# A hybrid trunk layer on one core: other planner prices, a later start for small parameters, halved state products, and FFN groups of 4, 6, 6 and 6

## The chip, the cores and the metric

One core of a Trainium2 chip runs the whole program in one launch. The metric is the device time in microseconds (us). Before the change three runs gave 1941.99, 1941.85 and 1940.84, a median of 1941.85. A separate profiled execution took 1942.22, of which the trace's span is 1940.5.

## The reference

One layer of a streaming encoder works on 640 tokens of width 1024: 512 prompt tokens of one request and 16 new tokens of each of 8 others, with the same weights:

```
x += 0.5 * swiglu(rmsnorm(x), w_ffn1_up, w_ffn1_down)      # up 1024 -> 2*2816, down 2816 -> 1024
P  = rmsnorm(x) @ w_in                                     # 1024 -> 10752 columns
A  = sliding-window attention, 16 heads, 4 kv heads, QK norm, a learned sink per head
B  = HGRN2 recurrence, 8 heads, state 128 x 128 per head and request
C  = causal conv(4) -> RG-LRU scan, times GeLU gate
x += (sig(gA)*A@w_attn_o + sig(gB)*B@w_hgrn_o + sig(gC)*C@w_lru_o) @ w_out
x += 0.5 * swiglu(rmsnorm(x), w_ffn2_up, w_ffn2_down)
```

Outputs are x, new keys and values, and the new HGRN2, convolution and RG-LRU states of both groups. All of it is float32. For HGRN2's sample requests the state update per head is `S = exp(b) * S + K^T V` over that request's 16 tokens.

## The kernel before

Activations lie transposed, features on the partitions and 640 tokens along the row, in two halves of 320. Every large product is taken three times: a weight is split into a high part `wh` and a remainder `wl` of the fast type (f32r), the activation likewise, and `wh`·high, `wh`·low, `wl`·high are added in PSUM (`proj`; the split is the cast in L717 and the subtraction in L718). So one 128-column block of weights takes 8 × 3 × 2 = 48 matmuls of 128x320. Small products (head products, HGRN2's, transposes in `tr`, L427) are plain f32 on the same engine; the program counts as a *kind* the type and the number of output rows.

The SwiGLU (`ffn`) runs over 22 blocks of 128 hidden columns. The first group of six computes gate and up plainly (2 × 48 = 96 matmuls a block). The later groups use seven products of combined halves in place of eight (`pair`, 84 matmuls a block), on sums and differences of the input that `combos` makes; `combos` is called after block 2 and finished at the end of the first group. After each group the down-projection goes over the 8 output blocks with the group's hidden blocks as contraction (`f0, nf` in the loop), and adds into x.

At the start `load_x` brings x in, transposes it, scales and splits it into `RA`; squares on ScalarE give the row sums, `first_rstd` the scale `RS`, which is applied after the first products. `load_params` brings the norm gains, biases and similar vectors as rows of one tile `AR`, transposes them once and copies them to `PRM`. `SK` holds the attention sinks, broadcast along the partitions by ten transfers; one DVE operation in `attention` negates them. `RA` and `RB` are the split operands of up- and down-projection.

The order is not the code's: every operation is put on a list with a priority (its position, `item`, less a `lag` for loads and splits), and `Sched.run` plays the five engines with modelled durations: the earliest start wins, ties within 0.04 go by priority, on ScalarE a function whose table isn't loaded pays `LOAD` after it has been picked. What comes out is one fixed program for each engine. An engine takes its instructions in that order, and a wait holds up all that stand behind it. DMAs go through SP's one queue.

Of the kernel before, what the change touches and what calls it, by code (L numbers as in the profile page):

```python
# [152 lines left out]
class Op:  # L153
    __slots__ = ("alts", "prio", "npred", "succ", "ready", "news", "bufs", "func", "dma", "done")


class Sched:
# [103 lines left out]
    def run(self):  # L261
# [3 lines left out]
        loaded, dma_free = "none", 0.0  # L265
# [70 lines left out]
def trunk_kernel(ctx: ExitStack, tc: tile.TileContext, A: dict, O: list):  # L336
# [65 lines left out]
    def dma(out, a, lag=None):  # L402
        v = out if isinstance(out, View) else a
        return S.op([("SP", 0.47, lambda: nc.sync.dma_start(ap_of(out), ap_of(a)))], [a], [out],  # L404
                    dma=v.n * 4 * v.proto.shape[0], lag=lag)

    def mm(calls):

        def cost(o, l, m):
# [11 lines left out]
        return S.op([("PE", dur, f)], [x for c in calls for x in c[1:3]], [c[0] for c in calls])  # L421

    def tr(calls):
# [5 lines left out]
        return S.op([("PE", sum(0.002 + 0.835e-3 * c[0].n for c in calls), f)], [x for c in calls for x in c[1:]], [c[0] for c in calls])  # L429
# [110 lines left out]

    def load_x():
        bs = S.buf("xs")
        xin = []
        for c in range(4):
            b = S.buf("x0")
            v = b.v.r("p (t d) -> p t d", t=4)
            dma(v, xp[:, :, c * 256:(c + 1) * 256], lag=(12, 2.5, 1.9, 1.8)[c])
# [4 lines left out]
        xv = X.v.r("p (k t) -> p k t", k=KD)
        for c in range(4):
# [31 lines left out]
    def load_params(names, r0, r1, lag=None):  # L585
        b = S.buf("pst")
        for name, r, c in (("norm_ffn1", 0, 8), ("norm_mix", 8, 8), ("norm_ffn2", 16, 8), ("conv_b", 24, 8),
                           ("conv_w", 32, 32), ("lru_b_a", 64, 8), ("lru_b_x", 72, 8), ("lru_lambda", 80, 8),
                           ("hgrn_lb_logits", 88, 8), ("hgrn_o_norm", 96, 1)):
            if name in names:  # L590
                src = A[name][0].rearrange("j (k p) -> (j k) p", p=P) if name == "conv_w" else A[name].rearrange("o (k p) -> (o k) p", p=P)
                dma(b[r - r0:r - r0 + c, 0:P].at(r), src, lag=lag)
        for r, name in ((97, "q_norm"), (98, "k_norm")):
            if name in names:
                for h in range(2):
                    dma(b[r - r0:r - r0 + 1, h * 64:h * 64 + 64].at((r, h)), A[name], lag=lag)
        ps = S.buf("ml")
        n = r1 - r0
        tr([(ps[:, :n], b[:n, :P], ident[:n, :n])])
        cp(PRM[:, r0:r1].at(r0), ps[:, :n], only=("DVE",))  # L600
# [257 lines left out]
    def ffn(wu, wd, norm, R, H, sfx, done, aside=()):  # L858
        ops = None
        for f0, nf in ((0, 6), (6, 8), (14, 8)):  # L860
            for f in range(nf):
# [16 lines left out]
            for m in range(KD):
# [338 lines left out]
    def hgrn():  # L1217
        mk = S.buf("msk")
        M1, BM, PM = mk[:, 0:32], mk[:, 112:120], mk[:, 120:122]
# [25 lines left out]
        S.op([("POOL", 0.2, lambda: nc.gpsimd.iota(il[:, 0:8](), [[-16, 8]], base=0, channel_multiplier=1))], (), [il[:, 0:8]])  # L1245
        ts(il[:, 0:8], il[:, 0:8], 4, ALU.arith_shift_right, only=one)
        ts(BM, il[:, 0:8], 0.0, ALU.is_equal, only=one)
# [14 lines left out]
        def head(i):  # L1262
# [186 lines left out]
```

## Time and profile before

| | |
|---|---|
| median of three runs | 1941.85 us |
| profiled execution | 1942.22 us, span 1940.5 us, mean granted clock 0.996 |
| TensorE (PE) | busy 1907.8 us, 98% |
| VectorE (DVE) | busy 1359.5 us, 70% |
| ScalarE (ACT) | busy 743.8 us, 38%, of which 127.0 us are 99 table loads |
| GpSimd (POOL) | busy 25.3 us |
| HBM traffic | 143.32 MB read, 10.63 MB written, 79 GB/s |

The profile gives busy time by engine, groups of equal instructions with their count and mean duration, the waits with what ended them, and a chain followed back from the last instruction. A matmul's record overlaps the next one's, so the time of one is read from the number in a full stretch and not from its own record. The granted clock is a share of full speed. With TensorE at 98%, places where it is idle, slow or does other work are what there is to find.

### The profile page before, as it was taken

The page shows a single profiled execution, that of the slowest core. Times are in us where ns is not written, and L with a number is a line of the kernel's source. Part 1 is how long each engine was busy: PE and PEld are TensorE (multiplying, and loading weights), DVE is VectorE, ACT ScalarE, POOL GpSimd, SP SyncE. Part 2 cuts the span into 40 slices and gives each one's busy share as a digit, 9 for nine tenths or more (in the row PEclk, how much of TensorE's full clock was granted, in tenths as well). Part 3 has the DMA queues.
Part 4 walks back from the last instruction along what each step waited for, and adds up shares of the span by engine and source line. Part 5 has one row for each costly group of instructions (what it writes and reads, how often), then busy time and mean ns, then how long its engine had stood idle before and what let it go on. Part 6 is the DMA issues. An engine that isn't in the chain of part 4 may idle for free.

```text
span 1940.5 us, 35075 instructions
## 1 busy us (share of the span) xinstructions
PE 1907.8 (98%) x14702; PEld 1862.7 (96%) x14702; DVE 1359.5 (70%) x2531; ACT 743.8 (38%) x1278; POOL 25.3 (1%) x58
## 2 busy tenths in 40 slices
PE   6999999999999999999999999999999999999999
PEld 5999999999999999989999999999999999999998
DVE  4957947866778783778547787886566867956963
ACT  4324513422478840887102343434212213412420
POOL 0000000000000000000000000000000000000000
PEclk9999999999999999999999999999999999999999
DMA  4223332234322212212322232222422223222322
GB/s 128 81 68 88 88 87 73 81 91 133 90 66 56 63 53 73 72 53 80 88 77 68 84 89 74 81 83 68 135 77 73 70 76 98 80 84 77 87 73 70
DMA packets 304440, 156.87 MB, mean 81 GB/s; under 512 B 22645, under 2 KB 301782, under 8 KB 304282
## 3 DMA queue, kind: packets, MB, share of 16 engines
q1 hardware_dynamic: 304282, 154.63, 27.6%
q8 instruction: 115, 1.88, 0.4%
q14 instruction: 43, 0.35, 0.1%
HBM read 143.32 MB, written 10.63 MB: 79 GB/s over the span
## 4 chain that ended last, share of the span: by engine, by line
PE 93%; DVE 3%; ACT 2%; SPq 1%; DMA 1%; issue 0%; DVEq 0%; ACTq 0%
PE pp L419 84%; PE me L419 4%; PE ml L419 3%; PE ml L427 1%; SPq L404 1%; PE me L427 1%; ACT L383 1%; DVE AR L373 1%; ACT AR L383 1%; DMA SK<-in_attn_sinks_dram 1%; DVE AR L359 1%; DVE wl L718 0%; DVE AR L1188 0%; DVE RB L359 0%; DVE wh L717 0%
## 5 line engine op out<-in xcount | busy, mean ns | idle before, releaser
L419 PE MATMUL pp<-RA,wh 128*128 128x320 f32 x4288 | 837.1, 315 | 4.2 <-DVE AR L359 3.9
L419 PEld LDWEIGHTS pp<-RA,wh 128*128 128x128 f32 x4288 | 674.8, 189 | 15.3 <-issue 7.6
L419 PE MATMUL pp<-RA,wl 128*128 128x320 f32 x2144 | 500.7, 310 | 1.1 <-DVE wl L718 1.1
L419 PE MATMUL pp<-RB,wh 128*128 128x320 f32 x2112 | 404.9, 309 | 1.4 <-DVE AR L359 0.9
L419 PEld LDWEIGHTS pp<-RA,wl 128*128 128x128 f32 x2144 | 362.6, 189 | 1.9 <-DVE wl L718 1.9
L419 PEld LDWEIGHTS pp<-RB,wh 128*128 128x128 f32 x2112 | 333.9, 188 | 2.2 <-DVE AR L359 1.4
L717 DVE CAST wh<-wr 128x1024 fp32r<-128x1024 f32 (+1 forms) x141 | 96.1, 681 | 265.6 <-PE pp L419 265.2
L419 PE MATMUL pp<-RB,wl 128*128 128x320 f32 x1056 | 250.8, 309 | 0.0
L718 DVE TENSOR_TENSOR wl<-wr,wh 128x1024 fp32r<-128x1024 f32 (+1 forms) x188 | 224.4, 1194 | 1.1 <-ACT wh L717 1.0
L419 PEld LDWEIGHTS pp<-RB,wl 128*128 128x128 f32 x1056 | 179.2, 188 | 0.0
L359 DVE TENSOR_TENSOR AR<-AR 128x640 f32<-128x640 f32 (+10 forms) x271 | 143.5, 534 | 27.1 <-ACT AR L383 20.6
L803 ACT CAST RW<-AR 128x512 fp32r<-128x512 f32 x160 | 98.3, 621 | 163.5 <-PE pp L419 109.5
L383 ACT ACTIVATE AR<-AR 128x640 f32<-128x640 f32 (+3 forms) x180 | 110.4, 614 | 85.0 <-DVE AR L359 76.9
L383 ACT ACT_TABLE_LOAD x99 | 127.0, 1283 | 11.5 <-DVE AR L359 9.4
L359 DVE TENSOR_TENSOR AR<-pp,AR 128x320 f32<-128x320 f32 x240 | 113.6, 485 | 22.3 <-PE pp L419 20.2
L419 PE MATMUL pp<-RX,RW 128*128 128x320 f32 x768 | 123.2, 309 | 0.0
L419 PEld LDWEIGHTS pp<-RX,RW 128*128 128x128 f32 x768 | 115.2, 188 | 0.0
L800 DVE TENSOR_TENSOR RW<-AR,RW 128x512 fp32r<-128x512 f32 x160 | 108.8, 685 | 1.0
L717 ACT CAST wh<-wr 128x1024 fp32r<-128x1024 f32 (+1 forms) x47 | 48.4, 1031 | 127.3 <-PE pp L419 127.3
L389 ACT COPY AR<-me 128x128 f32<-128x128 f32 (+3 forms) x73 | 26.2, 375 | 126.0 <-PE me L427 100.0
L373 DVE SCALAR_TENSOR_TENSOR AR<-pp,AR 128x320 f32<-128x320 f32 x96 | 45.9, 485 | 29.9 <-PE pp L419 29.9
L803 ACT CAST wh<-wr 128x1024 fp32r<-128x1024 f32 x32 | 33.6, 1051 | 77.1 <-PE pp L419 77.1
(184 smaller groups left out, 1930.5 us busy)
## 6 DMA issues: line engine op xcount, KB each, us to landing
wr<-in_w_in_dram SPq DMA_DIRECT2D x84, 512.0 KB
wr<-in_w_ffn_up_dram SPq DMA_DIRECT2D x56, 512.0 KB
AR<-in_w_ffn_up_dram SPq DMA_DIRECT2D x32, 512.0 KB
wr<-in_w_ffn_down_dram SPq DMA_DIRECT2D x32, 512.0 KB
wr<-in_w_ffn_down_dram SPq DMA_DIRECT2D x16, 384.0 KB
wr<-in_w_attn_o_dram SPq DMA_DIRECT2D x8, 512.0 KB
AR<-in_state_hgrn_dram SPq DMA_DIRECT2D x8, 512.0 KB
wr<-in_w_lru_o_dram SPq DMA_DIRECT2D x8, 512.0 KB
```

The costliest lines, as they stand in the source:

```text
L359: alts = [dve(out.n, lambda: nc.vector.tensor_tensor(out(), a(), b(), op=op))]
L373: return S.op([dve(out.n, lambda: nc.vector.scalar_tensor_tensor(out(), a(), ap_of(s), b(), op0=op0, op1=op1), isinstance(s, View))], [a, ...
L383: nc.scalar.activation(out(), a(), func, bias=ap_of(bias), scale=ap_of(scale), **kw)
L389: alts = [act(out.n, lambda: nc.scalar.copy(out(), a()), 0, a), dve(out.n * (1.0 if a.in_psum else 0.5), lambda: nc.vector.tensor_copy(out ...
L404: return S.op([("SP", 0.47, lambda: nc.sync.dma_start(ap_of(out), ap_of(a)))], [a], [out], dma=v.n * 4 * v.proto.shape[0], lag=lag)
L419: nc.tensor.matmul(o(), l(), m(), start=s, stop=e)
L427: nc.tensor.transpose(o(), i(), d())
L717: S.op([act(nk * P, lambda: nc.scalar.copy(h(), r())), dve(nk * P * 0.5, lambda: nc.vector.tensor_copy(h(), r()))], [r], [h], lag=2)
L718: S.op([dve(nk * P, lambda: nc.vector.tensor_tensor(l(), r(), h().bitcast(F32), op=ALU.subtract))], [r, h], [l], lag=1.5)
L800: S.op([dve(out.n, lambda: nc.vector.tensor_tensor(out(), a(), b(), op=op))], [a, b], [out], lag=lag)
L803: S.op([act(out.n, lambda: nc.scalar.copy(out(), a()))], [a], [out], lag=lag)
```

## The change

Planner: a ScalarE operation that needs a table load is now compared with the load's time in its start (before, it was added only afterwards). On TensorE an operation of another kind than the one before gets 0.3 of an item's priority as handicap, and modelled time for the change of kind. `S.late` lets one call give later priorities.

Start: x_sample goes with each quarter of x, the first gains go through ScalarE's DMA queue, the other parameters are loaded after `RS` is there, are issued at block 4 and transposed at block 8, and the sinks are loaded once `PRM` is there.

HGRN2: the masked values of a head's eight requests took 1024 columns with all 128 token rows; now 512 columns hold four requests in rows 0 to 63 and four in rows 64 to 127, and two products of 64 rows each replace two of 128 rows.

FFN: groups of 4, 6, 6, 6 in place of 6, 8, 8; `combos` is called after block 0, with later priority.

```diff
@@ Sched
+    TO_R = 0.09
+    RESIZE = 0.1
-        o.prio = self.item * 1e5 + self.seq if lag is None else (self.item - lag) * 1e5
+        o.prio = (self.item + self.late) * 1e5 + self.seq if lag is None else (self.item - lag) * 1e5
...
-                        cands.append((max(free[e], o.ready, at), o, slots))
+                        sw = e == "ACT" and o.func is not None and o.func not in tables[loaded]
+                        cands.append((max(free[e], o.ready, at) + (self.LOAD if sw else 0.0), o, slots))
...
+                    if e == "PE" and c[1].mode[0] != mode:
+                        return c[1].prio + 0.3 * 1e5
                     return c[1].prio + (0.35e5 if sw else 0.0)
...
-                start += self.LOAD
+            if e == "PE":
+                start += self.TO_R if o.mode[0][0] and not mode[0] else 0.0
+                start += self.RESIZE if o.mode[0][1] != mode[1] else 0.0
+                mode = o.mode[1]
@@ mm, cost
+            if l.proto.shape[0] == 64 and w == P and m.n == 512:
+                return 0.45
@@ load_x
-            dma(v, xp[:, :, c * 256:(c + 1) * 256], lag=(12, 2.5, 1.9, 1.8)[c])
+            lag = (12, 2.7, 2.6, 2.5)[c]
+            if c == 0:
+                load_params(("norm_ffn1",), 0, 8, lag=13, act=True)
+            dma(v, xp[:, :, c * 256:(c + 1) * 256], lag=lag)
+            dma(sv(bs, c), xs[:, c * 256:(c + 1) * 256], lag=lag)
@@ load_params
+        later = () if act else (RS.v,)
...
-                dma(b[r - r0:r - r0 + c, 0:P].at(r), src, lag=lag)
+                dma(b[r - r0:r - r0 + c, 0:P].at(r), src, lag=lag, after=later, act=act)
...
+        def place():
+            ps = S.buf("ml")
+            n = r1 - r0
+            tr([(ps[:, :n], b[:n, :P], ident[:n, :n])])
+            cp(PRM[:, r0:r1].at(r0), ps[:, :n], only=("DVE",))
@@ ffn
+    CHUNKS, ASIDE, LATE = ((0, 4), (4, 6), (10, 6), (16, 6)), 0, 4.0
-        for f0, nf in ((0, 6), (6, 8), (14, 8)):
+        for f0, nf in CHUNKS:
...
-                if f0 + f == 2:
+                if f0 + f == ASIDE:
+                    S.late = LATE
                     ops, rest = combos(norm, R, sfx)
+                    S.late = 0.0
...
-    ffn(A["w_ffn1_up"][0], A["w_ffn1_down"][0], G1, RA, RB, "", spill)
+    ffn(A["w_ffn1_up"][0], A["w_ffn1_down"][0], G1, RA, RB, "", spill, ((4, more_params), (8, lambda: place[0]())))
@@ attention
-            dma(SK[h * 64:h * 64 + 64, 0:8].at(h), sk[h:h + 1, :].to_broadcast([64, 8]))
+            dma(SK[h * 64:h * 64 + 64, 0:8].at(h), sk[h:h + 1, :].to_broadcast([64, 8]), after=(PRM.v,))
...
-                dma(SK[p0:p0 + 16, 8:16].at((b, h)), sk[h:h + 1, :].to_broadcast([16, 8]))
+                dma(SK[p0:p0 + 16, 8:16].at((b, h)), sk[h:h + 1, :].to_broadcast([16, 8]), after=(PRM.v,))
@@ hgrn
-            tt(Vb.v.r("p (b v) -> p b v", b=NB), Vt[:, TP:T].bc(1, P, NB, P), BM.bc(2, P, NB, P), ALU.mult)
+            tt(Vb.v.r("p (b v) -> p b v", b=4), Vt[:, TP:T].bc(1, P, 4, P), BM.bc(2, P, 4, P), ALU.mult)
...
+            pus = [S.buf("ml") for _ in range(2)]
+            mm([(pus[h].v, KT[h * 64:h * 64 + 64, TP:T], Vb[h * 64:h * 64 + 64, :], True, True) for h in range(2)])
             for h in range(2):
-                pu = S.buf("ml")
-                mm([(pu.v, KT[:, TP:T], Vb[:, h * 512:(h + 1) * 512], True, True)])
-                tt(S0[:, h * 512:(h + 1) * 512], S0[:, h * 512:(h + 1) * 512], pu.v, ALU.add)
+                tt(S0[:, h * 512:(h + 1) * 512], S0[:, h * 512:(h + 1) * 512], pus[h].v, ALU.add)
```

In the rows of order that follow, a name is the buffer written, `<-`, the buffers read; `wr`, `wh`, `wl` are a weight block as loaded, its high part and its remainder, `pp`, `me`, `ml` PSUM banks.

SP's queue at the program's beginning, in the kernel before:

```order
L404 DMA SK_73<-in_attn_sinks_dram 64x8x1
L404 DMA RX0_108<-in_x_prompt_dram 128x4x256
L404 DMA RX0_108<-in_x_sample_dram 128x1024
L404 DMA AR_74<-in_norm_ffn1_dram 8x128
L404 DMA wr0_79<-in_w_ffn1_up_dram 128x8x128
L404 DMA RX0_108<-in_x_prompt_dram 128x4x256
```

A sinks' transfer stands first, the other nine further down among the first weights. After the change the queue begins with x, and the sinks stand in the first FFN's first down-projection, between its weight blocks:

```order
L413 DMA wr0_79<-in_w_ffn1_down_dram 128x4x128
L413 DMA SK_73<-in_attn_sinks_dram 64x8x1
L413 DMA SK_73<-in_attn_sinks_dram 16x8x1 x4
L413 DMA SK_73<-in_attn_sinks_dram 64x8x1
L413 DMA SK_73<-in_attn_sinks_dram 16x8x1
L413 DMA wr1_80<-in_w_ffn1_down_dram 128x4x128
L413 DMA SK_73<-in_attn_sinks_dram 16x8x1 x3
L413 DMA wr2_81<-in_w_ffn1_down_dram 128x4x128
```

VectorE in the same down-projection after the change, where the operation on all ten sinks' transfers now stands:

```order
L382 SCALAR_TENSOR_TENSOR AR_74<-pp3_89,AR_74 128x320
L376 TENSOR_SCALAR AR_74<-AR_74 128x8
L368 TENSOR_TENSOR AR_74<-AR_74 128x8
L374 TENSOR_SCALAR SK_73<-SK_73 128x16
L374 TENSOR_SCALAR AR_74<-AR_74 128x8
L743 CAST wh0_82<-wr0_79 128x512
L382 SCALAR_TENSOR_TENSOR AR_74<-pp0_86,AR_74 128x320
L744 TENSOR_TENSOR wl0_84<-wr0_79,wh0_82 128x512
```

Before, the operation on SK stood in the start, ahead of most of the first group. Now a weight's split and the emptying of two banks stand behind it.

TensorE at one head's state update in HGRN2 before:

```order
L419 MATMUL ml1_93<-AR_74 128x128
L419 MATMUL ml1_93<-ident_64,AR_74 128x128
L419 MATMUL ml0_92<-AR_74 128x512
L419 MATMUL ml1_93<-AR_74 128x512
L419 MATMUL pp0_86<-RA_61,wh0_82 128x320
```

And after:

```order
L432 MATMUL ml0_92<-AR_74 128x128
L432 MATMUL ml0_92<-ident_64,AR_74 128x128
L432 MATMUL pp2_88<-RA_61,wh0_82 128x320
L432 MATMUL pp0_86<-RA_61,wh0_82 128x320
L432 MATMUL pp2_88<-RA_61,wh0_82 128x320
L432 MATMUL pp0_86<-RA_61,wh0_82 128x320
L432 MATMUL pp2_88<-RA_61,wl0_84 128x320
L432 MATMUL pp0_86<-RA_61,wl0_84 128x320
L432 MATMUL ml1_93<-AR_74 128x512
L432 MATMUL ml0_92<-AR_74 128x512
L432 MATMUL pp2_88<-RA_61,wh0_82 128x320
```

The two products of 512 columns are now of 64 rows each and stand by themselves between fast ones.

ScalarE in the RG-LRU, one stretch before:

```order
L383 ACT_TABLE_LOAD
L383 ACTIVATE AR_74<-AR_74,DER_69 128x640
L383 ACT_TABLE_LOAD
L383 ACTIVATE AR_74<-me0_90,PRM_68 128x320
L383 ACTIVATE AR_74<-AR_74 128x640
L383 ACT_TABLE_LOAD
L383 ACTIVATE AR_74<-AR_74 128x640
L383 ACT_TABLE_LOAD
L383 ACTIVATE AR_74<-AR_74 128x640
```

And after:

```order
L392 ACT_TABLE_LOAD
L392 ACTIVATE AR_74<-AR_74,DER_69 128x640
L392 ACTIVATE AR_74<-AR_74 128x640
L392 ACT_TABLE_LOAD
L392 ACTIVATE AR_74<-me0_90,PRM_68 128x320
L392 ACTIVATE AR_74<-me1_91,PRM_68 128x320
L392 ACTIVATE AR_74<-AR_74,DER_69 128x640
L392 ACTIVATE AR_74<-me0_90,PRM_68 128x320
```

Operations of one table stand together more often. Over the program the table loads go from 99 to 72, in the RG-LRU's stretch from 31 to 18; 128x320 matmuls go down by 48, and the visits to f32 work on TensorE from 193 to 173.

## Rows read from the trace of the kernel before

**Rows 1.** Page: busy time by engine, share of the span, instructions

```profile
PE 1907.8 (98%) x14702; PEld 1862.7 (96%) x14702; DVE 1359.5 (70%) x2531; ACT 743.8 (38%) x1278; POOL 25.3 (1%) x58
```

**Rows 2.** Windows, a dense stretch: bounds, length, busy (count) by engine, clock, DMA, GB/s

```profile
50.00:100.00 50.00, 50.00 (x343) 50.00 (x342) 42.69 (x75) 17.18 (x25) 0.00 (x0) 1.00 0.29 82
```

**Rows 3.** Waits of PE: who ended them, us in total, times, longest

```profile
PE me L427 <- DMA RX<-in_x_prompt_dram: 11.2, 2, 11.0
...
PE pp L419 <- DVE AR L359: 4.8, 3, 3.6
```

**Rows 4.** Timeline of SP's queue, start: begin, length, what is issued

```profile
0.73 0.73 SPq L404 DMA_DIRECT2D SK<-in_attn_sinks_dram  x1
...
15.35 4.82 SPq L404 DMA_DIRECT2D SK<-in_attn_sinks_dram  x6
```

**Rows 5.** DMA issues of the sinks: count, size of each

```profile
SK<-in_attn_sinks_dram SPq DMA_DIRECT2D x8, 0.5 KB
SK<-in_attn_sinks_dram SPq DMA_DIRECT2D x2, 2.0 KB
```

**Rows 6.** Windows of the start

```profile
2.00:6.00 4.00, 0.00 (x0) 0.00 (x0) 0.00 (x1) 0.02 (x1) 0.00 (x0) 1.00 0.04 0
6.00:20.00 14.00, 8.25 (x34) 6.79 (x35) 5.56 (x11) 8.39 (x25) 0.00 (x0) 1.00 0.96 293
20.00:28.00 8.00, 7.74 (x57) 7.39 (x55) 5.98 (x10) 7.94 (x23) 0.00 (x0) 1.00 0.10 12
34.00:40.00 6.00, 5.71 (x22) 5.75 (x23) 1.39 (x4) 1.30 (x6) 0.00 (x0) 0.50 0.33 92
```

**Rows 7.** Chain that ended last, the start: begin, length, what

```profile
19.54 9.68 DMA SK<-in_attn_sinks_dram
...
32.06 2.24 DMA SK<-in_attn_sinks_dram
```

**Rows 8.** Timeline of the start: ACT, PE and DVE, idle before and its releaser

```profile
10.92 0.42 ACT L383 ACTIVATE AR<-RX 128x256 f32<-128x256 f32 x1 [8.90 <-DMA RX<-in_x_prompt_dram]
...
34.28 0.38 PE L427 MATMUL ml<-ident,AR 91*128 91x91 f32 x1 [6.10 <-DMA SK<-in_attn_sinks_dram]
...
37.32 0.18 DVE L365 TENSOR_SCALAR SK<-SK 128x16 f32<-128x16 f32 x1 [2.36 <-DMA SK<-in_attn_sinks_dram]
```

**Rows 9.** Chain that ended last, one head's state update in HGRN2

```profile
1060.67 2.16 PE ml L419 x8
```

**Rows 10.** Groups of PE by form: count | busy, mean ns

```profile
L419 PE MATMUL ml<-AR 128*128 128x512 f32 x32 | 15.1, 593 | 0.0
L419 PE MATMUL ml<-AR 128*64 128x256 f32 x96 | 12.1, 388 | 0.0
```

**Rows 11.** Timeline of PE, a visit to 64 rows

```profile
496.87 0.33 PE L427 MATMUL ml<-ident,AR 64*128 64x64 f32 x2
```

**Rows 12.** Windows, the RG-LRU

```profile
790.00:900.00 110.00, 102.01 (x665) 100.24 (x664) 88.46 (x172) 95.73 (x118) 6.70 (x13) 0.97 0.22 62
```

**Rows 13.** Groups of ACT from 775 to 900 us: table loads

```profile
L383 ACT ACT_TABLE_LOAD x36 | 46.2, 1283 | 0.6
```

**Rows 14.** Timeline of PE, the RG-LRU's longest wait

```profile
847.36 0.71 PE L419 MATMUL pp<-RA,wh 128*128 128x320 f32 x3 [3.62 <-DVE AR L359]
```

**Rows 15.** Timeline of PE and DVE, end of the first FFN group

```profile
115.56 0.75 PE L419 MATMUL pp<-RB,wh 128*128 128x320 f32 x4
...
120.45 0.82 DVE L359 TENSOR_TENSOR RB<-AR,RB 128x640 fp32r<-128x640 f32 x1
```

**Rows 16.** Windows, the second group of the first FFN (pairs)

```profile
162.00:257.00 95.00, 95.00 (x649) 95.00 (x649) 82.60 (x141) 44.15 (x72) 0.00 (x0) 1.00 0.32 89
```

**Rows 17.** Timeline of PE and DVE, the last pair before a down-projection

```profile
170.94 0.45 PE L419 MATMUL pp<-RA,wh 128*128 128x320 f32 x2
...
173.97 0.83 DVE L359 TENSOR_TENSOR RB<-AR,RB 128x640 fp32r<-128x640 f32 x1 [0.85 <-ACT RB L389]
```

**Rows 18.** Page, costliest groups: the down-projection's adding into x

```profile
L373 DVE SCALAR_TENSOR_TENSOR AR<-pp,AR 128x320 f32<-128x320 f32 x96 | 45.9, 485 | 29.9 <-PE pp L419 29.9
```

More of the change, by code (lines that the diff above doesn't have):

```diff
@@ L153 @@
 class Op:
-    __slots__ = ("alts", "prio", "npred", "succ", "ready", "news", "bufs", "func", "dma", "done")
+    __slots__ = ("alts", "prio", "npred", "succ", "ready", "news", "bufs", "func", "dma", "done", "mode")
 class Sched:
@@ L164 @@
     LOAD = 1.35
+    TO_R = 0.09
+    RESIZE = 0.1
     def __init__(self):
         self.ops, self.tags = [], {}
-        self.item, self.seq = 0, 0
+        self.item, self.seq, self.late = 0, 0, 0.0
     def tag(self, name, slots, psum=False):
@@ L264, in run @@
         ready = {e: {} for e in engines}
-        loaded, dma_free = "none", 0.0
+        loaded, dma_free, mode = "none", 0.0, (True, P)
         tables = dict(TABLES, none=())
@@ L400, in fill, with dma @@
         return S.op(pick(alts, only), (), [out])
-    def dma(out, a, lag=None):
+    def dma(out, a, lag=None, after=(), act=False):
         v = out if isinstance(out, View) else a
-        return S.op([("SP", 0.47, lambda: nc.sync.dma_start(ap_of(out), ap_of(a)))], [a], [out],
-                    dma=v.n * 4 * v.proto.shape[0], lag=lag)
+        alts = [("SP", 0.47, lambda: nc.sync.dma_start(ap_of(out), ap_of(a)))]
+        if act:
+            alts = [("ACT", 0.47, lambda: nc.scalar.dma_start(ap_of(out), ap_of(a)))]
+        return S.op(alts, [a, *after], [out], dma=v.n * 4 * v.proto.shape[0], lag=lag)
     def mm(calls):
@@ L419, in f @@
                 nc.tensor.matmul(o(), l(), m(), start=s, stop=e)
-        return S.op([("PE", dur, f)], [x for c in calls for x in c[1:3]], [c[0] for c in calls])
+        modes = [(c[1].proto.dtype == F32R, c[0].proto.shape[0]) for c in (calls[0], calls[-1])]
+        return S.op([("PE", dur, f)], [x for c in calls for x in c[1:3]], [c[0] for c in calls], mode=modes)
     def tr(calls):
@@ L427, in f @@
                 nc.tensor.transpose(o(), i(), d())
-        return S.op([("PE", sum(0.002 + 0.835e-3 * c[0].n for c in calls), f)], [x for c in calls for x in c[1:]], [c[0] for c in calls])
+        return S.op([("PE", sum(0.002 + 0.835e-3 * c[0].n for c in calls), f)], [x for c in calls for x in c[1:]], [c[0] for c in calls],
+                    mode=[(False, P)] * 2)
     def fixed(name, shape, dt=F32):
@@ L558, in load_x @@
                 cp(xk(2 * c + h)[:, 0:TP], pa.v, only=("DVE", "ACT"))
-            tr([(pb[:, h * P:(h + 1) * P], bs[:, (2 * c + h) * P:(2 * c + h + 1) * P], ident.v) for h in range(2)])
+            tr([(pb[:, h * P:(h + 1) * P], sv(bs, c)[:, h * P:(h + 1) * P], ident.v) for h in range(2)])
             for h in range(2):
@@ L563, in load_x @@
         for c in range(4):
-            tiles = [xin[c][:, t, :] for t in range(4)] + [bs[:, c * 256:(c + 1) * 256]]
+            tiles = [xin[c][:, t, :] for t in range(4)] + [sv(bs, c)]
             for t in range(NT):
@@ L595, in load_params @@
                 for h in range(2):
[L596 to L600, printed above, removed]
+                    dma(b[r - r0:r - r0 + 1, h * 64:h * 64 + 64].at((r, h)), A[name], lag=lag, after=later)
+        def place():
[3 more added lines that the diff above has]
+            cp(PRM[:, r0:r1].at(r0), ps[:, :n], only=("DVE",))
+        if not act:
+            return place
+        place()
     G1, GM, G2, CVB, CVW, BA, BX, LAM, LBL, ON, QN, KN = 0, 8, 16, 24, 32, 64, 72, 80, 88, 96, 97, 98
@@ L881, in ffn @@
                     stt(o, p, 0.5, o, ALU.mult, ALU.add)
-                if f0 == 14:
+                if f0 + nf == 22:
                     done(m)
@@ L1244, in hgrn @@
             masks[h] = LV[:, s * 80:(s + 1) * 80].r("p (n h) -> p n h", h=h)
[L1245 to L1247 removed]
+        S.op([("POOL", 0.2, lambda: nc.gpsimd.iota(il[:, 0:4](), [[-16, 4]], base=64, channel_multiplier=1))], (), [il[:, 0:4]])
+        ts(il[:, 0:4], il[:, 0:4], 63, ALU.bitwise_and, 4, ALU.arith_shift_right, only=one)
+        ts(BM, il[:, 0:4], 0.0, ALU.is_equal, only=one)
         atts = [S.buf("hatt") for _ in range(2)]
```

20 lines of the change are left out of this document (11 added, 9 removed).

## The prediction

> **What bounds the kernel now.** The page comes first: TensorE is busy 1907.8 of 1940.5 us [rows 1], so nothing else sets the time except where TensorE is idle, slow, or doing other work than it must. A dense stretch among the windows gives the price of a matmul: 343 in 50 us, 0.1458 us each, at the full granted clock [rows 2]. At that price I look for the places that don't keep it. TensorE's waits name two large ones at the start, 11.0 us for x [rows 3] and 6.10 for the sinks [rows 8], and the RG-LRU [rows 3, 14]. The windows add what waits don't show: 22 matmuls in 6 us at clock 0.50 after the second of them [rows 6], where 41 would fit, and 665 in 110 us in the RG-LRU [rows 12], where 754 would. Everything else is close to dense, so removing matmuls is worth their full price, and delays elsewhere matter only if they reach TensorE.
>
> **The start: +11.2 us.** The sinks are broadcast element by element: 2 transfers of 2.0 KB and 8 of 0.5 KB [rows 5] are 512 and 128 pieces of 4 bytes, 2048 in all. One stands ahead of x in SP's queue [rows 4]; from 2 to 6 us nothing is moved to speak of (0 GB/s), then x comes at 293 [rows 6]. That is 4.1 us for 512 pieces, 8 ns a piece. Six transfers issued from 15.35 us on are 1152 pieces [rows 4] and take 9.68 us in the chain [rows 7], 8.4 ns a piece, and from 20 to 28 us the queues move 12 GB/s [rows 6]: while sinks are moved, little else is. TensorE's transposition of the parameters waits behind them, 6.10 us [rows 8], and then runs at half clock, 1.2 GHz in place of 2.4: (41 − 22) × 0.1458 = 2.8 us. All three go: 4.1 + 6.1 + 2.8 = 13.0. Late next is the row sum: ScalarE has 10 of its 20 squares behind the last split in place of 5, and a square is 0.42 us [rows 8], so up to 2.1 us; I take 1.8 off. The first gains on ScalarE's queue cost nothing, since ScalarE waits 8.90 us for x there [rows 8].
>
> *A page on this.* The Trainium skill, "DMA: Bandwidth & Descriptors", section "Rules for kernel authors", says that a last dimension that isn't contiguous becomes one descriptor per element. By it the price follows the sinks wherever they are put, and the rows agree (8 ns a piece, twice). It speaks against moving them into a weight stream.
>
> **48 matmuls fewer: +7.0.** A block done by `pair` takes 84 matmuls in place of 96, and two more blocks in each FFN are done so: 2 × 2 × 12 = 48, × 0.1458 = 7.0. They stand in dense stretches. The price is a fourth pass of adding into x, 32 operations of 0.485 us on VectorE [rows 18], 7.8 us in each FFN, spread over its length; VectorE has 12.4 us free of 95 in a pair stretch [rows 16], so I cost it at nothing there.
>
> **State products: +4.5.** The eight heads' updates are 32 records of 128x512; one head's four are most of the 2.16 us in the chain [rows 9, 10], which also holds four of 128x128: by columns 2048 of 2560, so 1.72, or 0.43 a record. Afterwards there are two records for each row half. If the halves run one after the other, the time stays 1.72, plus a visit to 64-row mode; the one visit in the trace, two tiny products, takes 0.33 us [rows 11], of which I take 0.3. That is 8 × −0.3 = −2.4. If they run together, 1.72 − 0.86 = 0.86 a head, at best 6.9 without the visit and 4.5 with it. The nearest row is that of column halves: 96 records of 128x256 with 64 columns take 12.1 us busy [rows 10], where 96 × 0.215 (half a 512) would be 20.6, so halves of the array do run together. I take 4.5 and keep −2.4 to 6.9.
>
> *A page on this.* The Trainium skill, "TensorEngine Tiling (Array Packing)", sections "Key Properties" and "Gotcha 1: PSUM Pressure", says that row tiles work independently if they write different PSUM banks, which `ml0` and `ml1` are, and that changing the mode drains the engine. By it the gain is the upper case less eight drains. No run here shows row halves of this size yet.
>
> **RG-LRU: +9.** What is lost there is (754 − 665) × 0.1458 = 13 us. ScalarE is busy 95.73 of the 110 us [rows 12], with 36 loads of 1.283 us from 775 to 900 [rows 13]; the order has 13 fewer in that stretch, 16.7 us, which brings ScalarE to 79. VectorE is then the busiest at 88.46, the share at which a pair stretch loses nothing (82.60 of 95, 649 matmuls) [rows 16]. What may stay is dependence, as in the wait of 3.62 us on a VectorE result [rows 14], and the scans are as long as before. Bounds 0 and 13; I take 9, since what waits there is fed by ScalarE. The loads saved elsewhere lie beside a ScalarE at 38% [rows 1]: nothing. The handicap for kinds leaves 20 fewer visits to f32 on TensorE; such visits of full width show in the trace only as their own work, so nothing too, with 0 to 2 us as bounds.
>
> **Sinks in the down-projection: −13.3.** This is the step that gives back most. Let U be the end of the first group's up products. The sinks are issued once `PRM` is written, which comes with the last work of that group on VectorE, about U + 5.8. By the order 1664 pieces go first (13.3 us at 8 ns), then a weight block (0.75), then 384 (3.1), and from the end of the last transfer in the chain, 34.30, to VectorE's operation, 37.32 [rows 7, 8], it was 3.0, of which I take 2.8: U + 25.8. VectorE reaches the operation on SK after the third block of the down-projection, at about U + 13, and waits; the waiting holds up the next weight's split and the next emptying. TensorE has one block in hand, 24 × 0.1458 = 3.5 us, and is out of work at U + 16.9. It goes on when seven VectorE operations behind SK are done, 1.7 us, at U + 27.5. That is 10.6 us idle, and 2.7 for the slow clock after it (as at 34 to 40 us, [rows 6]). Bounds: nothing, if pieces are spread better than before or VectorE comes later, and −18, if the parameters come late by 5 us too.
>
> **Groups of four: −5.8.** At the end of the first group the last product's gate, split and remainder take from 115.56 to 121.27 us [rows 15]. TensorE covers it with the down-projection's blocks that are ready: all but one, before 5 × 6 = 30 matmuls, 4.4 us, and all waits of that kind outside the RG-LRU together are 1.2 us [rows 3]. Now 3 × 6 = 18, 2.6 us. The chain being 4.4 to 5.7 long as TensorE sees it, 1.8 to 3.1 is uncovered: 2.4 in each FFN, and about 0.5 each for a slower clock. The later groups have 30 matmuls (4.4 us) for a chain of 170.94 to 174.80, 3.9 us [rows 17], before 42 (6.1 us): covered, by 0.5.
>
> **Sum.** 11.2 + 7.0 + 4.5 + 9 − 13.3 − 5.8 = 12.6 us, off the profiled execution's 1942.2 (0.4 above the median of 1941.85): 1929.5 us.
>
> **Rivals.**
> 1. *The sinks are hidden.* VectorE gets there later than I think, or pieces on an otherwise idle queue move faster. Against it: two rows at 8 ns, and an order that puts SK ahead of a split. Then 13.3 comes back: 1916. Chance 0.15.
> 2. *The RG-LRU does not shrink*, since what bounds it is the chain through VectorE. For it: VectorE at 80% there and the 3.62 us wait on it [rows 12, 14]; against it: the loads stand inside that chain. 1929.5 + 9 = 1938.5, within measurement of before. Chance 0.13.
> 3. *The other side: the later groups stall too.* Six junctions, three in each FFN, have a cover of 4.4 us for a chain of 3.9, and VectorE now does more adding. If its queue is late by 3 us, each junction loses 2.4, and 2.8 for the clock after it: 6 × 5.2 = 31, so 1961. It makes the change slower from 2.8 us a junction, about 0.5 + 2 us of lateness with part of the clock. Against it: VectorE is 13% free in such stretches [rows 16]. Chance 0.12.
> 4. *The change does not do what it says*: the planner's new prices make no difference outside the RG-LRU, and what it moves elsewhere gains a few us more. 0.05, faster.
>
> **The numbers.** My forecast has 0.55, with a range of its own of 1920 to 1938 (state products and RG-LRU at their ends, sinks between half and one and a half times their price). About 0.2%, 3.9 us, is what a measurement can tell from no change: below 1938.0 is faster, above 1945.7 slower. Faster: 0.55 + 0.15 + 0.05 = 0.75; same 0.13; slower 0.12. The range reaches from rival 1 to the edge of rival 2: 1915 to 1941.
>
> **What would show it.** Right: x's first use near 7 us in place of 11; no wait for sinks at 28; a wait of VectorE for SK of about 13 us in the first down-projection, with TensorE idle about 10 behind it and half clock after it; 2 to 3 us of idle at the first group's end in each FFN; 128x512 records that overlap; ScalarE's loads at 72 and more than 720 matmuls in the RG-LRU's 110 us. It would be wrong if VectorE's operation on SK waits under 3 us, if the RG-LRU still has idle times above 3 us, or if TensorE is idle at the ends of the later groups.

## The result and the profile after

Four runs of the changed kernel gave a median of 1931.58 us (1930.63 to 1932.32), four of the kernel before 1941.92: a ratio of 0.9945, 95% interval 0.9930 to 0.9961. The forecast was 1929.5, within 1915 to 1941. The profiled execution's span is 1929.1 us, 11.4 shorter than before. Its page, busy time by engine:

```profile
PE 1895.8 (98%) x14654; PEld 1851.0 (96%) x14654; DVE 1388.1 (72%) x2610; ACT 740.3 (38%) x1299; POOL 36.4 (2%) x63
```

TensorE does 48 matmuls less and is still busy 98% [rows 1]. What it waits for has changed places; its waits, to be set beside [rows 3]:

```profile
PE pp L432 <- DVE AR L382: 12.7, 2, 12.3
PE pp L432 <- DVE wl L744: 5.7, 5, 2.7
PE me L441 <- DMA RX<-in_x_prompt_dram: 4.1, 2, 2.0
PE me L432 <- DVE NL L368: 2.4, 1, 2.4
```

The 11.2 us for x are 4.1 now. TensorE's first use of x, and its use of the squares for the row sums (`SSQ`), which it takes without a wait:

```profile
4.57 1.97 PE L441 MATMUL me<-ident,RX 128*128 128x128 f32 x8 [2.05 <-DMA RX<-in_x_prompt_dram]
...
28.77 1.27 PE L432 MATMUL me<-ident,SSQ 128*128 128x128 f32 x10
```

A new wait of 12.3 us stands first. It is the sinks in the first down-projection, seen in the timeline of SP's queue, VectorE and TensorE (begin, length, what, idle before and its releaser):

```profile
77.28 4.85 SPq L413 DMA_DIRECT2D SK<-in_attn_sinks_dram  x7
82.23 0.39 SPq L413 DMA_DIRECT2D wr<-in_w_ffn_down_dram  x1
85.98 5.04 SPq L413 DMA_DIRECT2D SK<-in_attn_sinks_dram  x3
...
83.61 0.17 DVE L368 TENSOR_TENSOR AR<-AR 128x8 f32<-128x8 f32 x1
99.20 0.18 DVE L374 TENSOR_SCALAR SK<-SK 128x16 f32<-128x16 f32 x1 [15.42 <-DMA SK<-in_attn_sinks_dram]
...
72.13 0.75 PE L432 MATMUL pp<-RB,wh 128*128 128x320 f32 x4
...
87.70 0.46 PE L432 MATMUL pp<-RB,wl 128*128 128x320 f32 x2
100.44 0.64 PE L432 MATMUL pp<-RB,wh 128*128 128x320 f32 x1 [12.29 <-DVE AR L382]
```

The first group's products end at U = 72.13. VectorE comes to the sinks at U + 11.7 and goes on at U + 27.1; TensorE is out of work at U + 16.0 and back at U + 28.3. The forecast had U + 13, 25.8, 16.9 and 27.5. The windows of after (the columns of [rows 2]):

```profile
2.00:6.00 4.00, 1.67 (x8) 1.60 (x9) 0.44 (x2) 2.05 (x7) 0.00 (x0) 1.00 0.93 257
...
101.00:110.00 9.00, 8.64 (x49) 8.56 (x49) 7.72 (x29) 1.14 (x3) 0.00 (x0) 0.79 0.40 117
118.00:188.00 70.00, 70.00 (x479) 70.00 (x478) 61.41 (x104) 34.06 (x55) 0.00 (x0) 1.00 0.29 83
781.00:889.00 108.00, 102.13 (x667) 100.41 (x666) 86.72 (x164) 87.42 (x114) 19.21 (x21) 0.97 0.22 63
```

From 2 to 6 us x is moving, where nothing moved before [rows 6]. From 101 to 110 the granted clock is 0.79 after the idle time, and 49 matmuls are done where 61.7 fit: 1.9 us. The pairs of the second group, from 118 to 188, are as dense as before [rows 16]. The RG-LRU is not: 108 − 667 × 0.1458 = 10.8 us are lost, where [rows 12] lose 13.0.

### The profile page after: what moved, and what is told of

It is laid out like the page before. It is cut to its first block, busy times and chain, and to the rows that moved or that the text cites. A ratio compares the mean times of both kernels' runs of the same rounds, so it can differ in the third digit from the quotient of the medians.

```text
span 1929.1 us, 35224 instructions
## 1 busy us (share of the span) xinstructions
PE 1895.8 (98%) x14654; PEld 1851.0 (96%) x14654; DVE 1388.1 (72%) x2610; ACT 740.3 (38%) x1299; POOL 36.4 (2%) x63
## 2 busy tenths in 40 slices
DMA packets 305130, 156.89 MB, mean 81 GB/s; under 512 B 22949, under 2 KB 302598, under 8 KB 304970
## 4 chain that ended last, share of the span: by engine, by line
PE 94%; DVE 2%; DMA 1%; ACT 1%; issue 0%; SPq 0%; DVEq 0%; ACTq 0%
PE pp L432 85%; PE me L432 4%; PE ml L432 3%; PE ml L441 1%; PE me L441 1%; DMA SK<-in_attn_sinks_dram 1%; DVE AR L368 1%; ACT AR L392 1%; DVE AR L1222 0%; ACT L392 0%; DVE AR L382 0%; DMA RX<-in_x_prompt_dram 0%; SPq L413 0%; DVE wl L744 0%; DVE RB L368 0%
## 5 line engine op out<-in xcount | busy, mean ns | idle before, releaser
L432 PE MATMUL pp<-RA,wh 128*128 128x320 f32 x4192 | 813.1, 313 | 0.3 <-DVE AR L368 0.3
L432 PEld LDWEIGHTS pp<-RA,wh 128*128 128x128 f32 x4192 | 658.1, 188 | 12.5 <-issue 9.5
L432 PEld LDWEIGHTS pp<-RB,wh 128*128 128x128 f32 x2016 | 320.4, 188 | 14.8 <-DVE AR L382 13.3
L743 DVE CAST wh<-wr 128x1024 fp32r<-128x1024 f32 (+2 forms) x135 | 85.5, 633 | 237.5 <-PE pp L432 237.0
L744 DVE TENSOR_TENSOR wl<-wr,wh 128x1024 fp32r<-128x1024 f32 (+2 forms) x196 | 217.0, 1107 | 1.4 <-ACT wh L743 1.0
L368 DVE TENSOR_TENSOR AR<-AR 128x640 f32<-128x640 f32 (+12 forms) x271 | 139.5, 519 | 24.8 <-ACT AR L392 15.7
L392 ACT ACTIVATE AR<-AR 128x640 f32<-128x640 f32 (+2 forms) x184 | 110.6, 605 | 108.3 <-DVE AR L368 99.3
L743 ACT CAST wh<-wr 128x1024 fp32r<-128x1024 f32 (+2 forms) x61 | 59.7, 979 | 50.3 <-PE pp L432 49.9
L398 ACT COPY AR<-me 128x512 f32<-128x512 f32 (+3 forms) x74 | 26.8, 378 | 123.4 <-PE me L441 115.0
L382 DVE SCALAR_TENSOR_TENSOR AR<-pp,AR 128x320 f32<-128x320 f32 x128 | 61.4, 484 | 15.5 <-PE pp L432 15.5
L432 PE MATMUL pp<-RY,RW 128*128 128x320 f32 x432 | 69.2, 309 | 0.0
```

The costliest lines, as they stand in the source:

```text
L368: alts = [dve(out.n, lambda: nc.vector.tensor_tensor(out(), a(), b(), op=op))]
L382: return S.op([dve(out.n, lambda: nc.vector.scalar_tensor_tensor(out(), a(), ap_of(s), b(), op0=op0, op1=op1), isinstance(s, View))], [a, ...
L392: nc.scalar.activation(out(), a(), func, bias=ap_of(bias), scale=ap_of(scale), **kw)
L398: alts = [act(out.n, lambda: nc.scalar.copy(out(), a()), 0, a), dve(out.n * (1.0 if a.in_psum else 0.5), lambda: nc.vector.tensor_copy(out ...
L432: nc.tensor.matmul(o(), l(), m(), start=s, stop=e)
L743: S.op([act(nk * P, lambda: nc.scalar.copy(h(), r())), dve(nk * P * 0.5, lambda: nc.vector.tensor_copy(h(), r()))], [r], [h], lag=2)
```

## The experiments

They start from the changed kernel, but for one that starts from the kernel before. After the first of them, most are built on the version with contiguous sinks. Losses of a stretch are its length less its matmuls at 0.1458 us; where stages of different kinds are compared (attention, HGRN2, loads and kinds), less all kinds at the pitch that each has in dense stretches. One thing spreads all of them: the first group's products end between 72.7 and 74.3 us in the profiled executions of the nine versions with contiguous sinks and groups of four, whose first transfers have one order, and at 72.1 and 73.1 in the changed kernel and the one with the negation held back, which share another. So 1 to 2 us of any difference may come from when x lands. Three versions were timed in one execution only, and are marked so.

**Contiguous sinks.**

```diff
+    def sinks_load():
+        dma(SK[:, 0:16], A["attn_sinks"].to_broadcast([P, 16]))
...
+            cp(SK[:, 16 + h * 8:24 + h * 8].at(("d", h)), SK[:, 0:16].r("p (m two) -> p two m", two=2)[:, h, :], only=("DVE",))
...
+                dma(SK[p0:p0 + 16, 8:16].at((b, h)), SK[p0:p0 + 16, 16 + h * 8:24 + h * 8].at(("d", h)))
...
+        ts(SK[:, 16:32], SK[:, 0:16], -1.0, ALU.mult, only=("DVE",))
...
+    ffn(A["w_ffn1_up"][0], ... (10, sinks_load), (13, sinks_spread), (17, sinks_negate)))
...
-            dma(SK[h * 64:h * 64 + 64, 0:8].at(h), sk[h:h + 1, :].to_broadcast([64, 8]), after=(PRM.v,))
...
-                dma(SK[p0:p0 + 16, 8:16].at((b, h)), sk[h:h + 1, :].to_broadcast([16, 8]), after=(PRM.v,))
```

> The changed kernel, with the sinks loaded as 16 neighbouring floats to each partition (128 pieces in place of 2048) in the second FFN group, put in place by VectorE copies and eight small transfers within SBUF, and negated four blocks later. Theory A (the 15.42 us wait of VectorE for the element-wise sinks and the 12.3 us of idle TensorE behind it are the sinks' pieces alone): the idle at 88 us and the slow stretch after it go, 15 us, 1931.6 to 1916.5, within 1.5. Rival B (that place is late anyway, since weights and parameters come late after the first group): some 8 us of idle stays there, 1924 or more.

1918.02 us, ratio to before 0.9876 (0.9862 to 0.9891), 13.6 less than the changed kernel. No wait of TensorE is left between 80 and 460 us. Its transfers of the sinks:

```profile
SK<-SK SPq DMA_DIRECT2D x8, 0.5 KB
SK<-in_attn_sinks_dram SPq DMA_DIRECT2D x1, 8.0 KB
```

The calls stand at FFN blocks 10, 13 and 17, but the planner did not leave the work there. In the trace the sinks are the first thing on SP's queue, and all of it is done in the start:

```profile
0.74 0.40 SPq L413 DMA_DIRECT2D SK<-in_attn_sinks_dram  x1
...
11.30 6.95 SPq L413 DMA_DIRECT2D SK<-SK  x8
...
23.63 0.17 DVE L374 TENSOR_SCALAR SK<-SK 128x16 f32<-128x16 f32 x1
```

So this version changes the sinks' place as well as their pieces, and so do all that are built on it. The same 8 KB, as 128 pieces of 64 bytes and 128 of 32, cost at most a little in the new place: the first group's products end at 74.07, 1.9 us later than in the changed kernel, which is about the spread above. Behind the start the version gains 12.9 (the spans) + 1.9 = 14.8 us. Theory A, with the pieces told apart from the place by the kernel before, two runs further down.

**The negation alone held back** until the mixer's norm has written `RS`; the element-wise transfers stay.

```diff
-        ts(SK[:, 16:32], SK[:, 0:16], -1.0, ALU.mult, only=("DVE",))
+        S.op([dve(8, lambda: nc.vector.tensor_scalar(SK[:, 16:32](), SK[:, 0:16](), -1.0, None, op0=ALU.mult))],
+             [SK[:, 0:16], RS.v], [SK[:, 16:32]])
```

> The changed kernel with the element-wise sinks' transfers where they are; only VectorE's negation of them is held back until the mixer's norm. Theory A (what costs is that VectorE's queue is held): no idle near 88 us, about 1917. Rival B (the pieces themselves hold up the weight blocks behind them on SP's queue): TensorE is idle 8 to 11 us all the same, now waiting for weights, 1926 or so. By the queue's order two blocks are in hand and the last three come late by 3 to 5 us each, so I expect a share of both: 3 to 8 us idle, 1920 to 1925.

1926.49 (one execution), 5 us better than the changed kernel, past the end of what I expected and at rival B's time, with less idle than rival B's 8 to 11 us. VectorE's wait, and the timeline:

```profile
DVE wh L743 <- DMA wr<-in_w_ffn_down_dram: 9.4, 1, 9.4
```

```profile
98.08 0.43 DVE L743 CAST wh<-wr 128x512 fp32r<-128x512 f32 x1 [9.40 <-DMA wr<-in_w_ffn_down_dram]
...
98.96 0.63 PE L432 MATMUL pp<-RB,wh 128*128 128x320 f32 x1 [6.32 <-DVE AR L382]
```

The wait has changed its name and lost half its length: VectorE stands at the next weight block, which was issued behind the sinks. So two things cost here, the held VectorE and the pieces in front of the weights, and taking one away leaves about two thirds of the price (8.5 of 13.6 us).

**The kernel before with contiguous sinks**, by the same edit (its transfers have no `after`).

> The kernel before with nothing changed but the sinks, loaded as 16 neighbouring floats to each partition in the second FFN group. Theory A (the start's loss is the sinks' pieces: 4.1 us before x, 6.1 of waiting, 2.8 of slow clock): 1941.9 - 13 = 1929, the first matmul near 7 us in place of 11. Rival B (the changed kernel's start is better because of its new order of first transfers): not more than 6 us better, 1936 or more.

1929.36, ratio 0.9936 (0.9921 to 0.9951): one edit to the old kernel does what the whole change did. Here too the sinks are issued in the start, the first at 0.74 us as before [rows 4] and the small transfers from 10.20 on, so place and order are nearly those of before and the pieces are what differs. Windows of its start, its wait for x, and the end of the first group's products:

```profile
2.00:6.00 4.00, 0.20 (x1) 0.23 (x2) 0.58 (x5) 0.32 (x2) 0.00 (x0) 1.00 0.83 255
...
34.00:40.00 6.00, 6.00 (x44) 6.00 (x43) 5.77 (x14) 2.58 (x3) 0.00 (x0) 1.00 0.30 87
```

```profile
PE me L427 <- DMA RX<-in_x_prompt_dram: 6.2, 2, 5.8
```

```profile
102.93 0.75 PE L419 MATMUL pp<-RB,wh 128*128 128x320 f32 x4
```

The old start with this edit loses nothing at half clock [rows 6] and waits 5 us less for x, and its first group ends 12.6 us earlier than in [rows 15]. So some 12.6 of the 15.4 us that the changed kernel gains in the start were the sinks, and the new order of first transfers is worth what is left, about 3. Theory A.

**The scan's modelled time**, 0.73 to 1.42 us.

```diff
-                S.op([dve(T, lambda o=hs.v, ...
+                S.op([dve(1300, lambda o=hs.v, ...
```

> The changed kernel with contiguous sinks, and the planner's duration for the RG-LRU scan raised from 0.73 to 1.42 us (the trace has 1.49). Nothing else is changed. Theory A (what is left of the RG-LRU's loss, two stalls of 2.8 and 3.0 us with half clock after each, comes from VectorE running later than the plan, by 0.7 us a scan): one or both stalls go, 4 to 9 us, 1908 to 1912. Rival B (VectorE is simply too full there): within 1.5 us of the version with contiguous sinks alone.

1917.91 against 1918.02: no difference, theory A fell. The plan with the longer scan has the same stall of 2.4 us at the same remainder.

**The old rule for table loads.**

```diff
-                        cands.append((max(free[e], o.ready, at) + (self.LOAD if sw else 0.0), o, slots))
+                        cands.append((max(free[e], o.ready, at) + 0.0, o, slots))
...
+                start += self.LOAD
```

> The changed kernel with contiguous sinks (1918.0), and the planner's old rule for table loads on ScalarE: the load is again added only after the operation is picked. The order has 95 loads in place of 72, 31 in place of 18 in the RG-LRU. Theory A (VectorE ended the RG-LRU's waits, so 13 loads fewer there were worth about what the two traces differ by, 2.4 us): 1920 to 1921. Rival B (my forecast: 9 us in the RG-LRU): 1926 to 1927. The loads outside the RG-LRU are expected to be worth nothing by both.

1925.24 (0.9894 to 0.9927): 7.2 slower, near rival B's time, but not at its place. By stages, in the RG-LRU the loss is 1.7 larger, in attention 2.3, from HGRN2 to the second FFN 4.3; the start was 1.4 better.

**Old state products.**

```diff
-            tt(Vb.v.r("p (b v) -> p b v", b=4), Vt[:, TP:T].bc(1, P, 4, P), BM.bc(2, P, 4, P), ALU.mult)
+            tt(Vb.v.r("p (b v) -> p b v", b=NB), Vt[:, TP:T].bc(1, P, NB, P), BM.bc(2, P, NB, P), ALU.mult)
...
-            mm([(pus[h].v, KT[h * 64:h * 64 + 64, TP:T], Vb[h * 64:h * 64 + 64, :], True, True) for h in range(2)])
...
+                mm([(pu.v, KT[:, TP:T], Vb[:, h * 512:(h + 1) * 512], True, True)])
```

> The changed kernel with contiguous sinks, and HGRN2's state products as before (two products of 128 rows a head). Theory A (row halves run together: 2.16 us with the small products before, 1.26 in their own visit now): 8 x 0.47 = 3.7 us slower, 1921 to 1922. Rival B (the difference in that stretch comes from fewer visits to f32 work by the planner's kind rule): under 1 us slower.

1921.71 (one execution), 3.7 slower, with a start equal within 0.2 us. Theory A.

**Old groups.**

```diff
-    CHUNKS, ASIDE, LATE = ((0, 4), (4, 6), (10, 6), (16, 6)), 0, 4.0
+    CHUNKS, ASIDE, LATE = ((0, 6), (6, 8), (14, 8)), 2, 0.0
```

> The changed kernel with contiguous sinks, and the FFN's groups of 6, 8, 8 with the combinations called after block 2, as before. Theory A (48 matmuls at 0.1466 are 7.0 us, and the two stalls of 1.56 and 1.53 us at the end of the groups of four are the price): 7.0 - 3.1 = 3.9 slower, 1922. Rival B (the stalls come from the order and not from the short group, so they stay): 7 slower, 1925. Rival C (the fourth pass of adding costs VectorE time that reaches TensorE): less than 3 slower.

1921.04 (0.9874 to 0.9904), 3.0 slower, with the stalls at the group ends gone. By the times alone this lies between theory A's 3.9 and rival C's "less than 3". In the profiled executions the span is 2.8 longer with 1.2 less lost in the start, so 4.0 for the groups. With this correction it is theory A, and the fourth pass of adding costs nothing that shows.

**Later priorities for the RG-LRU's results.**

```diff
+                S.late = 3.0
                 tt(g.v, g.v, hss[i].v, ALU.mult)
                 parts(RB, m, g.v)
+                S.late = 0.0
```

> The changed kernel with contiguous sinks, and in the RG-LRU the gate products and the splits of the results get a priority three items later in the plan, so that VectorE makes the next block's remainders (NL, wl) first. No work is added or removed. Theory A (the stalls are an order on VectorE: urgent remainders behind work that nobody waits for): the 2.8 us stall for NL and most of the clock loss after it go, 3 to 6 us, 1912 to 1915. Rival B (VectorE is full there, so whatever is put off is missed later): 1918 within 1.5.

1914.97 (0.9842 to 0.9872), 3.0 better than contiguous sinks alone, of which some 1.3 are the start: in part theory A.

**A quarter of the scan.**

```diff
-                S.op([dve(T, lambda o=hs.v, a=a.v, t=t.v: ...
+                S.op([dve(T // 4, lambda o=hs[:, 0:T // 4], a=a[:, 0:T // 4], t=t[:, 0:T // 4]: ...
```

> The changed kernel with contiguous sinks, in which the RG-LRU's scan runs over 160 of 640 columns, planned so (it leaves out the recurrence of the other 480): 8 x 1.1 = 9 us less work on VectorE in a stretch of 112 us. Theory A (VectorE ends the RG-LRU's waits): TensorE's loss there falls from 10.5 us to 5 or less, 1912 or less. Rival B (ScalarE or the chain through both does): the loss stays within 2 us of 10.5, 1916 or more.

1913.89 (one execution), 4.1 better than contiguous sinks alone. The RG-LRU's windows, first with contiguous sinks, then with later priorities, then with the quarter scan:

```profile
764.00:876.00 112.00, 106.33 (x695) 103.96 (x694) 88.87 (x168) 89.58 (x118) 19.23 (x21) 0.97 0.22 62
```

```profile
762.00:875.00 113.00, 108.38 (x719) 106.72 (x719) 90.16 (x170) 89.64 (x119) 15.37 (x20) 0.98 0.22 64
```

```profile
762.00:872.00 110.00, 106.17 (x705) 104.74 (x704) 86.01 (x176) 89.42 (x117) 11.14 (x21) 0.98 0.23 66
```

Lost are 10.7, 8.2 and 7.2 us. Less work on VectorE, or the same work in a better order, gives back about 3; neither comes to theory A's 5. Of the 7.2 us that stay in the last, 3.7 are waits (2.6 of them ended by VectorE, 1.1 by ScalarE), and a mean clock of 0.98 over 110 us is some 2 more; what would remove them these runs do not settle.

**No rule for kinds**, and then **neither rule** (with the old load rule as well).

```diff
-    TO_R = 0.09
-    RESIZE = 0.1
+    TO_R = 0.0
+    RESIZE = 0.0
...
-                        return c[1].prio + 0.3 * 1e5
+                        return c[1].prio
```

> The changed kernel with contiguous sinks, and no handicap or modelled time for a change of kind on TensorE; the rule for table loads stays. The order has 183 visits to f32 work in place of 173 and 75 table loads in place of 72. Theory A (as forecast, full-width visits cost only their own work): 0 to 2 us slower, 1918 to 1920. Rival B (fewer visits save a mode change of 0.3 to 0.4 us each): 3 to 4 us slower, 1921 to 1922.

1916.49 (0.9853 to 0.9886) against 1918.02 (0.9862 to 0.9891), with 0.7 of the difference in the start: no slower; ten visits more to f32 work cost nothing. Theory A.

> The changed kernel with contiguous sinks and without both planner rules (kinds and table loads), so with the plan's prices of before. Without the load rule alone it took 1925.2, with losses 4.3 us larger from HGRN2 to the second FFN, 2.3 in attention, 1.7 in the RG-LRU. Theory A (the two rules act by themselves): 1925 plus what the kind rule is worth, 1925 to 1928. Rival B (the 4.3 us after the RG-LRU came from the kind rule without the load rule, not from the loads): 1921 to 1923.

1920.99 (0.9879 to 0.9908). Without the kind rule, the load rule is worth 1920.99 − 1916.49 = 4.5 us (2.5 of it in the RG-LRU, 1.1 after it, 0.7 in attention); with it 7.2. So rival B: the kind rule alone makes the order worse, by 4.2 us, and the load rule undoes that. Why it does was not looked into.

**Combinations put off further**, with the later priorities.

```diff
-    CHUNKS, ASIDE, LATE = ((0, 4), (4, 6), (10, 6), (16, 6)), 0, 4.0
+    CHUNKS, ASIDE, LATE = ((0, 4), (4, 6), (10, 6), (16, 6)), 0, 8.0
```

> The changed kernel with contiguous sinks and the RG-LRU's later priorities (1915.0), and the combinations put 8 items later in the plan in place of 4, so that they come behind the first group's last split. Theory A (the stall of 1.56 us at the end of each group of four is VectorE doing combinations first): one or both shrink, 1 to 2.5 us, 1912.5 to 1914. Rival B (the last product's own chain is that long, and putting the combinations off makes the first pairs late): 1915 or more.

1914.53 (0.9844 to 0.9873) against 1914.97, no difference, and TensorE's gaps at the two group ends, from the start of the last matmul before to the start of the next, are 1.41 and 1.52 us, where they were 1.56 and 1.53. Rival B, as far as the time goes. With these two versions the kernel is 1.4% faster than before and 0.9% faster than the change.

## Why the prediction was right, step by step

| step | forecast | measured | from |
|---|---|---|---|
| start | +11.2 | +15.4 | 115.56 − 72.13 less 192 matmuls |
| 48 matmuls | +7.0 | +7.0 | groups as before: +4.0 net |
| state products | +4.5 | +3.7 | undone: 3.7 slower |
| RG-LRU | +9 | +2.2 | 13.0 − 10.8 lost |
| sinks | −13.3 | −14.6 | 12.3 idle, 2.3 from 100.44 to 110 us (9.56 − 50 × 0.1458) |
| groups of four | −5.8 | −2.8 | gaps of 1.56 and 1.53 from start to start, less a matmul each |
| sum | 12.6 | 10.9 | spans: 11.4 |

The remaining 0.5 is spread over attention and HGRN2.

**Start and sinks** went by the mechanism. The start was mis-sized by 4.2 us: x is first used at 4.57 us, 6.4 earlier than before where I had 4.1, and the 1.8 I took off for late squares did not come, since TensorE takes their sums at 28.77 without a wait. The sinks came near the forecast, 14.6 by the trace and 14.8 behind the start by the version with contiguous sinks. The price of 8 to 9 us per thousand pieces held where they were moved to (the last one landed 21.7 us after the first was issued, forecast 20.0; the 0.75 in that sum for a weight block was worked out from no row), as did the effect that a queue with 4-byte pieces does little else. The rule of the Trainium skill, "DMA: Bandwidth & Descriptors", section "Rules for kernel authors", that a non-contiguous last dimension costs a descriptor per element, agrees: with contiguous sinks the trace has 1808 packets under 512 B fewer (22949 to 21141, and 22645 to 20837 in the kernel before), where 2048 pieces became 256. What I had too simple is the holder. I named VectorE's place in the queue; the run with the negation held back shows that the weights behind the pieces would have stopped TensorE anyway, 6.3 us of 12.3 plus the slow clock.

**State products.** The groups and the timeline of after, one head:

```profile
L432 PE MATMUL ml<-AR 64*128 64x512 f32 x32 | 9.0, 641 | 0.0
```

```profile
1056.66 0.46 PE L432 MATMUL pp<-RA,wl 128*128 128x320 f32 x2
1057.05 1.13 PE L432 MATMUL ml<-AR 64*128 64x512 f32 x4
1058.11 0.86 PE L432 MATMUL pp<-RA,wh 128*128 128x320 f32 x4
```

32 records of 641 ns lie in 9.0 us of busy time, where [rows 10] have 15.1 for 593 ns: the halves run together. From the end of the fast matmul before (1057.12) to the end of the first one after (1058.97 − 3 × 0.146 = 1058.53) is 1.41, less that matmul 1.26 us. If the work is 0.86 (an estimate: two records of 0.43, from [rows 9]), the visit is 0.40; I had taken 0.3. The nearest row, of column halves, was the right one to go by.

**RG-LRU: the step that failed.** I took 9 of 13 us because ScalarE's loads were inside the waiting chain and VectorE's 80% was no more than a pair stretch bears; 2.2 came, and 667 matmuls in 108 us, where more than 720 in 110 were to show me right. Loads fell as the order said:

```profile
L392 ACT ACT_TABLE_LOAD x22 | 28.2, 1283 | 0.4
```

from 36 [rows 13], but what ends the long waits is VectorE. It already was before: of 7.9 us of waits there VectorE ended 5.5 and ScalarE 2.4. VectorE's own waits for ScalarE fell only from 27.0 to 23.9 us. Its timeline in front of one of the two long waits of after, and TensorE's at both:

```profile
799.18 1.49 DVE L1222 TENSOR_TENSOR_SCAN AR<-AR 128x640 f32<-128x640 f32 x1
800.59 0.15 DVE L368 TENSOR_TENSOR AR<-AR,HIST 128x8 f32<-128x8 f32 x1
800.64 0.23 DVE L382 SCALAR_TENSOR_TENSOR AR<-HIST,PRM,AR 128x8 f32<-128x8 f32 x1
800.78 1.49 DVE L1222 TENSOR_TENSOR_SCAN AR<-AR 128x640 f32<-128x640 f32 x1
802.19 1.54 DVE L368 TENSOR_TENSOR AR<-AR 128x640 f32<-128x640 f32 x2
803.64 0.82 DVE L368 TENSOR_TENSOR NL<-AR,NH 128x640 fp32r<-128x640 f32 x1
...
804.52 0.63 PE L432 MATMUL me<-NL,BH 128*128 128x320 f32 x1 [2.41 <-DVE NL L368]
...
834.43 0.56 PE L432 MATMUL pp<-RA,wl 128*128 128x320 f32 x2 [2.72 <-DVE wl L744]
```

VectorE has no gap here: two scans, two products nobody waits for, then the remainder that TensorE stands for. In front of the other wait it has none for 10 us. A mean of 80% over 110 us hid stretches of 100%. The rule for loads was worth 4.5 to 7.2 us in all, but only 2.5 and 1.7 of that in the RG-LRU; the rest lies in places where I had put nothing because ScalarE's mean is 38%. Less work on VectorE, or a better order there, gave back 2.5 to 3.5 us, so VectorE holds a part of the loss, and the cause of the rest is open. That the sum came out is in part luck: the start's surplus of 4 and 3 us less for the groups of four paid for the 6.8 missing here.

**Groups of four.** Half the size, and no slow clock followed (1.00 from 77 to 82 and from 1546 to 1551 us). TensorE's two waits at the ends of the first groups:

```profile
76.89 0.41 PE L432 MATMUL pp<-RB,wl 128*128 128x320 f32 x1 [1.25 <-DVE wl L744]
...
1546.06 0.56 PE L432 MATMUL pp<-RA,wl 128*128 128x320 f32 x2 [1.22 <-DVE wl L744]
```

They were ended by a weight's remainder, not by the last product's split, whose chain was covered better than I took from [rows 15].

**The rivals.** Sinks hidden: no. The RG-LRU not shrinking: mostly so, at 2.2 of 9. Later groups stalling: no, they show no wait, though in the pairs VectorE has no more room than I reckoned with, 8.6 us free of 70, 12%, where [rows 16] have 13%.

## What to carry to other kernels

A small transfer with a stride in its last dimension is priced by its pieces, and everything behind it in the queue pays, so moving it only moves the bill: load it contiguous and rearrange it on chip. What a removed wait is worth is read from the engine that would end it next, in the few microseconds before the wait, not from busy shares over a stage. An in-order engine needs urgent work ahead of work that nobody waits for; in the RG-LRU a priority of three items gave 2.5 us and leaving out three quarters of the scan's work 3.5.

## Hardware behaviour that was not expected

- Two f32 products of 64 rows and 512 columns, on the two row halves and into two PSUM banks, took 1.26 us with the visit to that mode, where the full-height pair took 1.72 (its share by columns of 2.16); undoing it cost 3.7 us over eight heads. By the estimate above the pair itself takes 0.86 and the visit 0.40.
- Ten visits more to full-width f32 products (183 in place of 173) cost nothing: 1916.49 against 1918.02.
- After 12.3 us without work TensorE had a granted clock of 0.79 from 101 to 110 us; after two idle times of 1.25 and 1.22 us it was 1.00, and after the wait of 2.72 us in the RG-LRU 0.66 from 835 to 840.
- 2048 pieces of 4 bytes, with one weight block between them, took one queue 21.7 us from the first issue to the last landing; the same 8 KB in rows of 64 bytes, and 4 KB more in rows of 32, cost the start some 2 us at most.
